# One pass of row sums moved into ScalarE's own order, and the place where the bound's broadcast line is read

## The chip, the cores and the metric

The kernel runs on one core of a Trainium2 chip. The time is device microseconds of the whole program, the median of several runs; lower is better. TensorE does the matrix products, VectorE and ScalarE the element work, GpSimd (POOL in the profile) a part of it and some DMA issues, SyncE (SP) most DMA issues.

## The reference, cut to what matters

A decoder trunk of two layers over 1024 tokens of width 1024, in float32.

```python
for layer in range(2):
    # layer 0: causal pooling; layer 1: forgetting attention over shared K/V
    h = x @ w_in                       # columns [main | mem q | main gate | mem gate]
    y = concat([main_fn(u) * silu(g_main), memory_attention(q_mem, mem, w_mem_kv) * silu(g_mem)])
    x = layer_norm(ALPHA * x + y @ w_out, ln_g, ln_b)
```

What the change touches lies in the output projection `y @ w_out` of layer 0, in the norm that follows it, and in the first part of layer 1, where the queries of its memory attention are made. In layer 1's forgetting attention the kernel scales q and k by powers of two before they become pairs of half-precision numbers. That scale needs an upper bound: the largest sum of absolute weights over 32 weight pieces (the key weights and layer 1's query weights), times a bound of the norm's output.

## The kernel before, in words

Each float32 product is made of three cheaper ones: an operand is split into a high part (`hi_lo`, line 163, on ScalarE), a low part (line 164, on VectorE, which needs the high part) and a rounded copy of the whole, "top" (line 165, on ScalarE).

**The output projection of layer 0** (`OutProj.rest`, lines 515 to 539) runs over four blocks of 256 tokens (`sp`), and in each over three groups of channels (`c` = 2, 0, 1). I call the twelve steps pieces 0 to 11: pieces 0 to 2 are the first block, 3 to 5 the second, and so on. A piece loads its activations from DRAM (line 533), splits them (lines 163 to 165, tiles `T`, six buffers shared by source, high and low/top) and then makes 48 products of 512 columns (line 496): two groups of 128 tokens by two halves of the columns, each a PSUM bank (`L`, three buffers, or `pj`, two) into which all three pieces of the block add. After the third piece VectorE reads the banks out (line 550) and the norm follows (`norm`, lines 541 to 566). Its rows are then transposed on TensorE for layer 1: 16 transposes per block (line 347), one behind every sixth product of the second and third piece of the block that follows (line 537). Four of them fill a PSUM bank `T` (two buffers), which lines 163 to 165 read out into `A`.

**The sums** (`look_ahead`, lines 190 to 202) are made meanwhile. Called from the loop of the products, it keeps three weight pieces on their way (line 194, a DMA issued by GpSimd into the ring `raw`, four buffers) and adds up the oldest one (line 200, an activation with an accumulator on ScalarE). Before the change it is called behind every 12th product, 32 times in all, and its activation is wrapped in an ordering relative to that product; a relation that the tool adds only to instructions on the product's own engine, TensorE. The order of ScalarE's queue is thus left to the scheduler. After the last piece `spread_bound` (lines 220 to 227) takes the largest per partition (line 223, VectorE), writes that column to DRAM (line 224, GpSimd) and reads it back as a row broadcast to all partitions (line 226, GpSimd) into a tile of the ring `raw`.

**The scales** (`scales_of`, lines 229 to 239) are ten small VectorE instructions; the first reads the broadcast row. In the code it is called in layer 1 behind the first head's queries (line 378), while the scheduler is free to place it.

The order on each engine's queue is the scheduler's, except on TensorE where parts are scheduled by hand, and where `keep_in_program_order` pins an instruction behind whatever was traced before it on its own engine. Each engine works off its queue in order: what stands behind a waiting instruction waits too.

Of the kernel before, what the change touches and what calls it, by code (L numbers as in the profile page):

```python
# [14 lines left out]
AF = mybir.ActivationFunctionType  # L15
ALU = mybir.AluOpType
AX = mybir.AxisListType

P = 128
# [54 lines left out]
def trunk_kernel(ctx, tc, x, xT, memT, win, wk, wv0, wv, wmk, wmv, wout, poolw, pscale, lng, lnb, bforget, out):  # L74
# [5 lines left out]
    nc = tc.nc  # L80
# [14 lines left out]
    def nm(tag):  # L95
        count[0] += 1
        return f"{tag}{count[0]}"

    def sb(shape, tag, bufs, dt=F32, where=None):
        return (where or pool).tile(shape, dt, tag=tag, name=nm(tag), bufs=bufs)  # L100
# [13 lines left out]
    def raw(shape):  # L114
        return sb(list(shape), "raw", 4)
# [38 lines left out]
    def three(a, b):  # L154
        return (a.hi, b.hi), (a.top, b.lo), (a.lo, b.top)
# [30 lines left out]
    rowsums = const.tile([P, NPIECES], F32, name="rowsums")  # L186
    to_see = [w[p, pc] for p in range(8) for w in (wk, win[1]) for pc in range(2)]
    landed, bound = [], []

    def look_ahead(after=None):  # L190

        while to_see and len(landed) < 3:
            r = raw([P, 4, P])
            nc.gpsimd.dma_start(r, to_see.pop(0))  # L194
            landed.append(r)
        if landed:
            k = NPIECES - len(to_see) - len(landed)
            r = landed.pop(0)
            with tc.issue_after(after):
                nc.scalar.activation(r, r, AF.Abs, accum_out=rowsums[:, k : k + 1])  # L200
        if not to_see and not landed and not bound:
            bound.append(spread_bound())

    scales = const.tile([P, 8], F32, name="scales")
    ex, ew, sq, unq, sqk, nsqk, tmp, tmp2 = (scales[:, k : k + 1] for k in range(8))

    def power_of(to, m, least):

        nc.vector.tensor_scalar(m, m, least, None, ALU.max)
        nc.vector.tensor_scalar(to.bitcast(I32), m.bitcast(I32), 0x7F800000, None, ALU.bitwise_and)  # L210
# [9 lines left out]
    def spread_bound():  # L220

        line = dram.tile([P, 1], F32, name=nm("line"))
        nc.vector.tensor_reduce(tmp, rowsums, AX.X, ALU.max)
        nc.gpsimd.dma_start(line, tmp)
        every = raw([P, P])
        nc.gpsimd.dma_start(every, line.rearrange("p o -> (p o)").partition_broadcast(P))
        return every

    def scales_of(every):

        nc.vector.tensor_reduce(tmp2, every, AX.X, ALU.max)
        power_of(ew, tmp2, 2.0 ** -24)
        nc.vector.tensor_tensor(ew, ew, ex, ALU.mult)
        nc.vector.reciprocal(sqk, ew)
        nc.vector.tensor_scalar(nsqk, sqk, -(2.0 ** 8), None, ALU.mult)
        nc.vector.tensor_scalar(sqk, sqk, 2.0 ** 8, None, ALU.mult)
        nc.vector.tensor_tensor(unq, ew, ew, ALU.mult)
        nc.vector.tensor_scalar(unq, unq, 2.0 ** -19, None, ALU.mult)
        nc.vector.reciprocal(sq, unq)
# [122 lines left out]
    def mem_attention(l, X, kv, qtile, ytile, yd):  # L362
# [6 lines left out]
        for h in range(MH):  # L369
            while turns:  # L370
                spread()
            q = parts_of(qtile, [P, S])
            run(slab(win[l, 8 + h], X, lambda cols, acc: hi_lo(q[:, cols], acc)))
            qs.append(q)
            if not l:
                keys(h)
            elif h == 0:
                scales_of(bound.pop())
            vals(h)
# [61 lines left out]
    class OutProj:  # L441
# [39 lines left out]
        def products(self, accs, c, ys, apart=False):  # L481

            high, low_top = (0,), (1, 2)
            if apart:
                order = [(a, nh, part) for a in range(2) for part in (high, low_top) for nh in range(2)]
            else:
                order = [
                    (a, nh, part) for part in ((low_top, high) if c == 0 else (high, low_top))
                    for a in range(2) for nh in range(2)
                ]  # L490
            for a, nh, part in order:
                for i in part:
                    for k in range(4):
                        kt = 4 * c + k
                        y, w = three(ys[:, k, a * P : (a + 1) * P], self.ws[nh][kt // 2][kt % 2])[i]
                        mm = nc.tensor.matmul(  # L496
                            accs[a][nh], y, w, start=kt == 8 and i == 0, stop=kt == 7 and i == 2,
                        )
                        self.done += 1
                        if not self.l and self.done % 12 == 7 and not bound:  # L500
                            look_ahead(mm.ins)
                        yield NH

        def early(self, y, ys):
# [592 lines left out]
```

## Time and profile before

| what | value |
|---|---|
| median of 3 runs | 1238.59 us (1235.18 to 1239.75) |
| the profiled execution's own time | 1231.11 us |
| span of its profile, first to last instruction | 1229.3 us |
| TensorE matmul busy | 1189.1 us, 97% of the span |
| VectorE busy | 781.2 us, 64% |
| ScalarE busy | 702.3 us, 57% |
| GpSimd busy | 239.2 us, 19% |
| mean granted TensorE clock | 0.99 |

The profile is of one execution, 7.5 us faster than the median of the three others. A row of its timeline gives the start, the duration, the engine, the line, the operation with its tiles and the count of merged instructions; in brackets stands how long the engine was idle before, and what released it. A row of a table by stretch gives the busy time of each engine in it, the granted clock (1.00 is full speed) and the share of the DMA engines.

### The profile page before, as it was taken

Reading aid. Unit: us, or ns where it says so; the run is one execution under the profiler, and the core shown is the slowest. Engines: PE = TensorE matmul, PEld = TensorE weight load, DVE = VectorE, ACT = ScalarE, POOL = GpSimd, SP = SyncE. Lnnn points to the kernel's source line nnn. Section 1 sums busy time; section 2 is a strip of 40 time slices with the busy share of each in tenths; the row PEclk is TensorE's granted clock in tenths of the full one; section 3 lists DMA queues with packets and bytes.
Section 4 is the critical chain, followed back from the end, with each engine's and each line's share of the span. In section 5 each row is a group of like instructions: output and inputs, shape, how many; then the busy total and the mean of one; then the engine's idle time right before and its main releaser. Section 6 shows DMA issues by size and latency. Waiting matters only on the chain. (4 is left out here: it accounts for less than half of the span.)

```text
span 1229.3 us, 20184 instructions
## 1 busy us (share of the span) xinstructions
PE 1189.1 (97%) x7018; PEld 729.0 (59%) x7018; DVE 781.2 (64%) x1839; ACT 702.3 (57%) x1508; POOL 239.2 (19%) x383
## 2 busy tenths in 40 slices
PE   8999999999988999999999999999999999999996
PEld 4566666555544566666786555556556555555553
DVE  7534676375724566346735787777877788774744
ACT  6555774374574335558623677666766676685220
POOL 4000000000031000000001444544444434650000
PEclk8999999999998999999999999999999999999999
DMA  6233564232586333326535799997998999996340
GB/s 224 86 115 93 121 136 137 86 121 95 185 279 188 129 120 101 102 85 123 109 112 120 166 174 198 200 175 165 205 201 161 207 185 222 233 232 212 131 142 35
DMA packets 272997, 187.79 MB, mean 153 GB/s; under 512 B 213424, under 2 KB 226864, under 8 KB 272896
## 3 DMA queue, kind: packets, MB, share of 16 engines
q1 hardware_dynamic: 270272, 178.06, 57.8%
q0 software_dynamic: 2624, 8.46, 2.1%
q8 instruction: 55, 0.90, 0.3%
q14 instruction: 46, 0.38, 0.1%
HBM read 103.43 MB, written 22.61 MB: 103 GB/s over the span
## 5 line engine op out<-in xcount | busy, mean ns | idle before, releaser
L267 PE MATMUL pj<-A,w 128*128 128x512 bf16 (+1 forms) x2928 | 690.0, 392 | 2.6 <-ACT A L163 2.3
L267 PEld LDWEIGHTS <-w 128*128 128x128 bf16 x1984 | 187.9, 98 | 221.0 <-issue 18.9
L267 PEld LDWEIGHTS pj<-A,w 128*128 128x128 f32 x976 | 180.9, 189 | 47.5 <-ACT A L163 3.9
L866 ACT ACTIVATE T<-MK,s 128x512 f32<-128x512 f32 x192 | 111.5, 581 | 54.1 <-DVE s L858 39.2
L888 DVE SCALAR_TENSOR_TENSOR P<-T,s,P 128x512 f16<-128x512 f32 x192 | 111.8, 613 | 39.6 <-ACT P L887 38.7
L887 ACT ACTIVATE P<-T,s 128x512 f16<-128x512 f32 x192 | 102.4, 576 | 59.6 <-issue 27.9
L164 DVE TENSOR_TENSOR w<-raw,w 128x512 bf16<-128x512 f32 x106 | 75.0, 709 | 83.2 <-PE pj L267 50.7
L496 PEld LDWEIGHTS <-T 128*128 128x128 bf16 x736 | 70.7, 98 | 83.8 <-issue 3.7
L244 PE MATMUL L<-B,B 128*128 128x512 f16 (+3 forms) x384 | 84.2, 327 | 6.3 <-DVE s L858 2.6
L858 DVE CUSTOM_DVE_ANT_0 MK<-L,R,scales 128x512 f32<-128x512 f32 (+3 forms) x128 | 80.3, 627 | 11.8 <-DMA R<-cumd 6.5
L163 ACT CAST w<-raw 128x512 fp32r<-128x512 f32 x106 | 65.9, 622 | 26.5 <-PE pj L267 14.5
L158 POOL TENSOR_SCALAR w<-raw 128x512 fp32r<-128x512 f32 x108 | 66.4, 622 | 71.7 <-DMA B<-B 44.9
L165 ACT CAST w<-raw 128x512 bf16<-128x512 f32 x106 | 65.8, 621 | 20.3 <-PE pj L267 19.7
L850 POOL TENSOR_SCALAR_AFFINE_SELECT R<-R 128x128 f32<-128x128 f32 x128 | 41.5, 330 | 164.4 <-DVE s L858 95.2
L169 POOL TENSOR_TENSOR w<-raw,w 128x512 bf16<-128x512 f32 x54 | 69.5, 1286 | 19.5 <-PE pj L267 17.3
L194 POOL DMA_DIRECT2D raw<-in_wk_dram x16 | 8.9, 559 | 330.4 <-DMA y0d<-Y 313.6
L164 DVE TENSOR_TENSOR T<-T,T 128x1024 bf16<-128x1024 f32 x23 | 28.0, 1217 | 66.6 <-ACT T L163 52.1
L244 PEld LDWEIGHTS <-B 128*128 128x128 f16 x384 | 34.0, 98 | 49.8 <-issue 12.7
L910 PE MATMUL O<-T,V 128*64 128x128 f16 (+1 forms) x1152 | 57.6, 220 | 4.5 <-DMA T<-P 4.2
L910 PEld LDWEIGHTS <-V 128*64 128x64 f16 (+1 forms) x1152 | 50.3, 104 | 18.3 <-issue 6.9
L496 PE MATMUL pj<-B,T 128*128 128x512 bf16 (+1 forms) x192 | 54.3, 392 | 4.5 <-DVE G L550 4.5
L163 ACT CAST T<-T 128x1024 fp32r<-128x1024 f32 x23 | 24.0, 1044 | 46.9 <-DMA T<-y1d 32.4
(250 smaller groups left out, 1710.0 us busy)
## 6 DMA issues: line engine op xcount, KB each, us to landing
raw<-in_win_dram SPq DMA_DIRECT2D x96, 256.0 KB, 2.8
raw<-in_wout_dram SPq DMA_DIRECT2D x40, 256.0 KB, 2.8
B<-B SPq DMA_DIRECT2D x69, 128.0 KB, 3.2
R<-cumd SPq DMA_DIRECT2D x16, 512.0 KB, 4.3
y0d<-Y SPq DMA_DIRECT2D x12, 512.0 KB, 2.9
T<-y0d SPq DMA_DIRECT2D x12, 512.0 KB, 4.9
T<-y1d SPq DMA_DIRECT2D x11, 512.0 KB, 4.6
raw<-in_wmk_dram SPq DMA_DIRECT2D x16, 256.0 KB, 2.6
```

The costliest lines, as they stand in the source:

```text
L158: nc.gpsimd.tensor_scalar(to, src, 1.0, 1.0, ALU.mult, ALU.mult)
L163: pin(nc.scalar.copy(to.hi, src))
L164: pin(nc.vector.tensor_tensor(to.lo, src, to.hi.bitcast(F32), ALU.subtract))
L169: nc.gpsimd.tensor_tensor(to.lo, src, to.hi.bitcast(F32), ALU.subtract)
L244: nc.tensor.matmul(acc, a, b, start=i == 0, stop=i == len(terms) - 1)
L267: nc.tensor.matmul(accs[n], a[:, k, :], b[:, pc * 4 + k, n * NH : (n + 1) * NH], start=seen[n] == 1, stop=seen[n] == 3 * KT,)
L496: mm = nc.tensor.matmul(accs[a][nh], y, w, start=kt == 8 and i == 0, stop=kt == 7 and i == 2,)
L858: nc.vector.tensor_tensor_reduce(p[:, lo:up], lg, R[:, lo:up], unq, top, ALU.add, ALU.min, m[:, n : n + 1])
L866: nc.scalar.activation(e, p[:, lo:up], AF.Exp, bias=top, scale=-1.0, accum_out=sums[:, n, hd % 2, i : i + 1],)
L887: nc.scalar.activation(pair[:, lo:up], e, AF.Copy, scale=r)
L888: nc.vector.scalar_tensor_tensor(pair[:, L + lo : L + up], e, r, pair[:, lo:up], ALU.mult, ALU.subtract)
L910: nc.tensor.matmul(acc[rows, (i % 4) * P : (i % 4) * P + P], v[:, b, 2 * j : 2 * j + (1 if e else 2), :].rearrange("p e d -> p (e d)"), pt ...
```

## The change

Three edits, and no instruction more or less on any engine.

1. The sums are called behind every 16th product in place of every 12th, and each is pinned on ScalarE behind what was traced there before it (`keep_in_program_order` in place of `issue_after`).
2. The broadcast row lands in the ring `P` (four buffers, used by the norm's two vectors here and by the memory's softmax later) in place of the ring `raw`.
3. The first instruction of `scales_of` is pinned on VectorE behind what was traced before it, which is the first head's queries of layer 1's memory attention.

```diff
-    def look_ahead(after=None):
+    def look_ahead():
...
-            with tc.issue_after(after):
-                nc.scalar.activation(r, r, AF.Abs, accum_out=rowsums[:, k : k + 1])
+            tc.keep_in_program_order(nc.scalar.activation(r, r, AF.Abs, accum_out=rowsums[:, k : k + 1]))
...
         nc.gpsimd.dma_start(line, tmp)
-        every = raw([P, P])
+        every = sb([P, P], "P", 4)
         nc.gpsimd.dma_start(every, line.rearrange("p o -> (p o)").partition_broadcast(P))
...
     def scales_of(every):
-        nc.vector.tensor_reduce(tmp2, every, AX.X, ALU.max)
+        tc.keep_in_program_order(nc.vector.tensor_reduce(tmp2, every, AX.X, ALU.max))
...
-                        mm = nc.tensor.matmul(
+                        nc.tensor.matmul(
                             accs[a][nh], y, w, start=kt == 8 and i == 0, stop=kt == 7 and i == 2,
                         )
                         self.done += 1
-                        if not self.l and self.done % 12 == 7 and not bound:
-                            look_ahead(mm.ins)
+                        if not self.l and self.done % 16 == 7 and not bound:
+                            look_ahead()
                         yield NH
```

In the built program the change of order reaches from the first output-projection pieces to layer 1's first queries: ScalarE's queue between its 356th and 428th instruction, VectorE's between its 375th and 538th, and with them the order of some of SyncE's and GpSimd's DMA issues. TensorE's queue is the same, instruction by instruction, and behind that stretch all queues are the same too.

## The prediction

> **What bounds the kernel now.** I read the page first, then the table by stretch around the output projection of layer 0, then the timelines of the engines there.
>
> ```profile
> span 1229.3 us, 20184 instructions
> PE 1189.1 (97%) x7018; PEld 729.0 (59%) x7018; DVE 781.2 (64%) x1839; ACT 702.3 (57%) x1508; POOL 239.2 (19%) x383
> ```
>
> TensorE has work 97% of the span and no other engine comes near it. So the time is TensorE's products plus the places where it stands still or runs slowly. By stretch:
>
> ```profile
> 364.00:375.00 11.00, 6.47 (x20) 4.22 (x19) 6.55 (x10) 7.48 (x19) 3.83 (x7) 0.69 0.76 248
> 394.00:405.00 11.00, 4.34 (x14) 3.10 (x13) 3.78 (x13) 2.02 (x3) 0.55 (x1) 0.69 0.27 75
> 413.00:447.00 34.00, 34.00 (x164) 20.25 (x163) 19.17 (x36) 11.24 (x17) 0.00 (x0) 1.00 0.33 108
> 481.00:505.00 24.00, 20.05 (x141) 14.62 (x141) 16.18 (x34) 16.81 (x37) 0.00 (x0) 1.00 0.40 133
> ```
>
> The columns behind the stretch are its length, then the busy time of PE, PEld, DVE, ACT and POOL, the granted clock and the DMA share. Two stretches have holes, and in both the clock is down to 0.69; later the same kind of work fills 34.00 of 34.00. TensorE's timeline gives what the holes cost:
>
> ```profile
> 363.71 1.27 PE L496 MATMUL L<-B,T 128*128 128x512 f32 x4
> 369.51 2.08 PE L496 MATMUL pj<-B,T 128*128 128x512 f32 x4 [4.53 <-DVE G L550]
> 371.38 1.91 PE L496 MATMUL L<-B,T 128*128 128x512 f32 x4
> 373.09 1.62 PE L496 MATMUL pj<-B,T 128*128 128x512 f32 x4
> ...
> 381.47 0.59 PE L496 MATMUL L<-W,T 128*128 128x512 bf16 x2
> ...
> 392.86 0.71 PE L496 MATMUL L<-Y,T 128*128 128x512 f32 x2
> ...
> 401.13 0.47 PE L347 MATMUL T<-ident,G 128*128 128x128 f32 x1 [6.66 <-ACT A L165]
> ...
> 412.88 1.18 PE L496 MATMUL L<-B,T 128*128 128x512 f32 x4
> ...
> 423.68 0.59 PE L496 MATMUL L<-W,T 128*128 128x512 bf16 x2
> ...
> 435.06 0.71 PE L496 MATMUL L<-Y,T 128*128 128x512 f32 x2
> ...
> 446.56 1.18 PE L496 MATMUL L<-B,T 128*128 128x512 f32 x4
> ```
>
> These are starts of pieces: 3 at 363.71, 4 at 381.47, 5 at 392.86, 6 at 412.88, 7 at 423.68, 8 at 435.06, 9 at 446.56. Piece 3 takes 17.76 us, its undisturbed twin 6 takes 10.80: **6.96 lost**. Piece 5 takes 20.02, its twin 8 11.50: **8.52 lost**. Piece 4 takes 11.39 against piece 7's 11.38: nothing. The change can give back at most 15.5 us here. The row 481 to 505 has 3.95 us of further holes, on layer 1's first weights; the change moves nothing there.
>
> **Why piece 5 stops.**
>
> ```profile
> 385.16 0.19 DVE L223 TENSOR_REDUCE scales<-rowsums 128x1 f32<-128x32 f32 x1 [0.63 <-ACT raw L200]
> 398.37 0.29 DVE L231 TENSOR_REDUCE scales<-raw 128x1 f32<-128x128 f32 x1 [13.03 <-DMA raw<-line]
> ...
> 399.79 0.67 DVE L164 TENSOR_TENSOR A<-T,A 128x512 bf16<-128x512 f32 x1
> ...
> 400.50 0.58 ACT L165 CAST A<-T 128x512 bf16<-128x512 f32 x1 [11.07 <-DVE A L164]
> ...
> 385.75 0.54 POOL L224 DMA_DIRECT2D line<-scales  x1 [4.95 <-DVE scales L223]
> 395.24 0.55 POOL L226 DMA_DIRECT2D raw<-line  x1 [8.94 <-issue]
> ```
>
> The scheduler put the scales' first instruction right behind the reduction whose result has to go to DRAM and back. VectorE waits 13.03 us for the row (385.75 out, 395.24 back, 398.37 landed). Behind it stands line 164 of a transposed bank, at 399.79, behind that ScalarE's line 165 at 400.50, which frees the bank, and TensorE's next transpose, at 401.13, needs the bank.
>
> **Why piece 3 stops.**
>
> ```profile
> 355.18 1.04 ACT L163 CAST T<-T 128x1024 fp32r<-128x1024 f32 x1
> ...
> 357.36 1.03 ACT L165 CAST T<-T 128x1024 bf16<-128x1024 f32 x1
> ...
> 364.63 0.63 ACT L200 ACTIVATE raw<-raw 128x512 f32<-128x512 f32 x1 [2.86 <-DMA raw<-in_wk_dram]
> ...
> 365.26 1.03 ACT L163 CAST T<-T 128x1024 fp32r<-128x1024 f32 x1
> ...
> 356.25 1.23 DVE L164 TENSOR_TENSOR T<-T,T 128x1024 bf16<-128x1024 f32 x1 [4.71 <-ACT T L163]
> 366.32 1.23 DVE L164 TENSOR_TENSOR T<-T,T 128x1024 bf16<-128x1024 f32 x1 [8.84 <-ACT T L163]
> ...
> 368.79 0.67 DVE L550 SCALAR_TENSOR_TENSOR G<-G,pj 128x512 f32<-128x512 f32 x1
> ...
> 372.32 0.68 DVE L550 SCALAR_TENSOR_TENSOR G<-G,pj 128x512 f32<-128x512 f32 x1
> ...
> 358.41 0.52 SPq L533 DMA_DIRECT2D T<-y0d  x1
> ```
>
> The banks `pj` of block 0 are read out at 368.79 and 372.32, behind a line 164 for piece 4 that waited 8.84 us for ScalarE's high part at 365.26. That high part waited for its source, issued at 358.41, as soon as piece 3's top (357.36 + 1.03) had freed the buffer, and at the end for a sum that itself waited 2.86 us for its weights.
>
> **The change part by part.** By the order of the built program:
>
> *The scales (edit 3)* move behind line 164 of the first head's queries, in layer 1, and VectorE goes from the norm straight to the transposed banks. The 13.03 us wait goes. What is late next: the bank, filled when piece 4 ends, waits for at most four sums, two casts and its own three copies. Sums, casts and the landing of their loads:
>
> ```profile
> L200 ACT ACTIVATE raw<-raw 128x512 f32<-128x512 f32 x32 | 20.0, 626 | 15.2 <-DMA raw<-in_wk_dram 8.2 <-DMA raw<-in_win_dram 6.9
> L200 ACT ACTIVATION_READ_ACCUMULATOR raw<-raw 128x1 f32 x32 | 6.0, 186 | 0.0
> DMA to landing us min/median/max: 2.8/3.4/7.3
> DMA to landing us min/median/max: 5.2/6.0/8.4
> ```
>
> (The third row is of the sums' loads, line 194; the fourth of the loads into `T` between 340 and 372 us.) A sum costs ScalarE 626 + 186 ns = 0.81 us. A bank holds four transposes, one behind every sixth product, and there are two: the second is full 24 products (5.7 us at 11.50/48) behind the first and is needed again 30 products (7.2 us) later. From the first bank's filling ScalarE and VectorE copy it (0.58 + 0.67 + 0.58), add the first sum (0.81), which frees the buffer for the fourth's load (0.55 to issue, 3.4 to land), and add the fourth (0.81): 7.4 us, 1.7 behind the second bank's filling. Then come that bank's own copies and a cast between them, 1.83 + 1.04. Together 4.6 of the 7.2: no stop. **Saved: 8.5 us**. With the slowest landing of the row, 7.3 in place of 3.4, it would be 1.3 less.
>
> At its new place the ten instructions take 399.79 - 398.37 = 1.42 us, in front of the read-out of head 0's values:
>
> ```profile
> 513.59 0.48 DVE L338 SCALAR_TENSOR_TENSOR MK<-pj,s,MK 128x256 f16<-128x256 f32 x1 [0.54 <-ACT MK L337]
> 510.97 10.84 PE L267 MATMUL pj<-A,w 128*128 128x512 f32 x48
> ```
>
> That read-out ends at 514.07, and the bank is needed at the second half of the 48 products, 510.97 + 5.42 = 516.39. With 1.42 added 0.9 us are left: cost nothing. The row has landed long before: its DMAs, 13 us as above, are issued at the end of block 2, three pieces (33.7 us) and layer 1's first weights ahead. Without that cover: up to 1.4 us.
>
> *The sums (edit 1).* One fewer stands ahead of piece 3's high part, and none between it and its top. The high part comes at 355.18 - 0.81 = 354.4; line 164 follows it by 1.07 and takes 1.23 (rows at 355.18 and 356.25), so the source buffer is free at 356.7 in place of 358.4. I take the median landing, 6.0: piece 4's high part starts at **362.7** in place of 365.26. The three sums in front of it are no hindrance (3 x 0.81, on loads that I count as issued by 355 and landed 3.4 later). From there the rows count on: the second `pj` bank was free for TensorE 373.09 - 365.26 = 7.83 later, and then 36 of the 48 products are left, 36 x 10.80/48 = 8.1 at full speed. Piece 4 starts at 362.7 + 7.83 + 8.1 = 378.6 in place of 381.47. **Saved: 2.8**; with a landing of 5.2 it is 3.6, with 8.4 it is 0.4. I take off 0.1 for a reciprocal that now stands ahead of the second read-out: 2.7.
>
> The other sums spread over pieces 4 to 9. Some 20 x 0.81 = 16.2 us come to ScalarE, over some 70 us of which in the undisturbed part 11.24 of 34 were busy. Each stands behind work that the next step needs anyway. The banks `pj` at the ends of blocks 1 and 2 hang on VectorE behind ScalarE's copies; adding up the same durations I find about 1 us of slack and take nothing, bounds 0 and +1 each. The memory's tokens load later than before (their buffers are the sums'), still ahead of their first cast.
>
> *The ring (edit 2).* `P` has a free buffer at that time (weights in one, the norm's vectors in two), so the row waits for none; and the tokens' fourth load no longer waits for the scales. Nothing.
>
> Sum: -8.5 - 2.7 = **-11.2 us**. For the profiled execution, 1231.11, that is 1219.9; its lead of 7.5 us on the median of the three runs is no part of the change, so I forecast 1238.59 - 11.2 = **1227.4**.
>
> **The clock.** In the trace holes of 4.53 and 6.66 us are followed by 0.69, while the stretch of 3.95 us in several holes kept 1.00. My piece 3 has two holes left, from 364.98 (363.71 + 1.27) to 362.7 + 4.25 = 366.95 (the first bank, 369.51 - 365.26 later) and, two groups of 0.9 later, from 368.75 to 370.5: 2.0 and 1.8, so I take full speed. [...]
>
> **The rivals.**
> 1. *Piece 3 stays cold.* The group behind the last hole then takes what such a group took, 373.09 - 371.38 = 1.71 in place of 0.9, and the next as much. Price 0.8 to 1.6: 1228 to 1229. [...] Against: 1.00 at 481 to 505.
> 2. *Half the gain goes into new waits of ScalarE.* Each of some 20 sums can wait for its load with casts behind it. At the slow landing a bank is 1.3 late (above); at five banks and two block ends that is 9.1: 1227.4 + 9.1 = 1236.5, within 0.5% of before. For it: sums waited 15.2 us for loads in all. Against: those loads ran behind each other at a DMA share of 0.76; spread out they meet 0.33.
> 3. *The stop of piece 3 repeats (slower).* It was a cast behind a waiting sum, with the banks' read-out behind that. Pinned sums now stand ahead of casts at the ends of all blocks. If that holds line 550 at three ends of blocks, at 6.96 each with the cold clock, 20.9 come back against 8.5 saved: 1238.59 + 12.4 = 1251. It decides from where a load takes longer than its lead, three sums of 16 products, 10.8 us. Against: the longest took 7.3.
> 4. *It doesn't do what it says*: pins that the scheduler evades. The built order excludes it for the scales; small, and counted with rival 2.
>
> **How the numbers follow.** Half a percent, 6.2 us, is about what a measurement of this kernel tells from no change. Chances: forecast 0.66, rival 1 0.10, rivals 2 and 4 0.17, of which a third still saves over 6.2, rival 3 0.07. So faster 0.82, same 0.11, slower 0.07. The range takes the landing from 5.2 to 8.4 (-12.0 to -8.8), the runs' spread (-3.4, +1.2), and reaches into rival 2: 1223 to 1235.
>
> **What would show it.** In the profile of the changed kernel: the scales' first reduction behind 490 us with no wait for the row; piece 5 in about 11.5 us; no transpose that waits for line 165; piece 3 in about 14.9 with two holes under 2.3 us and a clock near 1.00; no `pj` wait at the ends of blocks 1 and 2. Wrong would be: ScalarE idle on weights with line 163 behind it, and TensorE waiting for a bank at pieces 6, 9 or at 481 us.

## The result, and the profile after

The changed kernel takes **1220.70 us** (median of 4 runs, 1218.72 to 1226.01) against 1238.77 for the kernel before beside it (4 runs, 1235.18 to 1239.75): ratio 0.9866, 95% interval 0.9829 to 0.9903. The forecast was 1227.4 with a range down to 1223.0: the direction is right, the gain of 18.1 us is larger than the 11.2 forecast, and the time lies 2.3 us below the range. The two profiled executions differ by less, 9.95 us (1231.11 to 1221.16).

The page of the changed kernel:

```profile
span 1219.4 us, 20174 instructions
PE 1186.1 (97%) x7018; PEld 726.4 (60%) x7018; DVE 781.4 (64%) x1839; ACT 701.2 (57%) x1508; POOL 238.8 (20%) x383
```

The counts on the five engines are those of before; the ten instructions fewer in the first row are among those that do not count as busy.

The same stretches as in the prediction's table (length, busy time of PE, PEld, DVE, ACT, POOL, granted clock, DMA share, GB/s):

```profile
364.00:375.00 11.00, 9.93 (x45) 5.59 (x44) 10.86 (x22) 6.11 (x13) 2.12 (x4) 1.00 0.39 143
394.00:405.00 11.00, 11.00 (x54) 6.59 (x52) 10.29 (x21) 6.02 (x14) 1.64 (x3) 1.00 0.49 172
413.00:447.00 34.00, 34.00 (x164) 20.26 (x162) 19.01 (x34) 16.39 (x33) 2.73 (x5) 1.00 0.51 137
481.00:505.00 24.00, 22.63 (x126) 14.40 (x126) 10.78 (x31) 13.71 (x28) 0.00 (x0) 1.00 0.36 109
```

Of the two stops one hole of 1.07 us is left, and the clock of 0.69 is gone. The undisturbed stretch is still full with ScalarE at 16.39 instead of 11.24: part of the sums now lies there. TensorE's timeline, starts of pieces 3 to 6:

```profile
365.59 1.27 PE L495 MATMUL L<-B,T 128*128 128x512 f32 x4
369.75 1.20 PE L495 MATMUL pj<-B,T 128*128 128x512 f32 x4 [1.07 <-DVE G L549]
377.71 0.59 PE L495 MATMUL L<-W,T 128*128 128x512 bf16 x2
389.09 0.71 PE L495 MATMUL L<-Y,T 128*128 128x512 f32 x2
400.59 1.18 PE L495 MATMUL L<-B,T 128*128 128x512 f32 x4
```

Piece 3 takes 12.12 us (17.76 before), piece 5 11.50 (20.02). But piece 3 starts 1.88 us later than before (365.59 against 363.71). That is no sign of a cost: in three further profiles of the kernel before, pieces 0 to 2 are as slow as here (first column of the table below), and its first profile is the exception. The scales are read far behind, with no wait in brackets:

```profile
497.41 0.28 DVE L230 TENSOR_REDUCE scales<-P 128x1 f32<-128x128 f32 x1
```

From the starts, piece 6 begins 12.29 us earlier (412.88 to 400.59), and the spans differ by 9.9. Of the 2.4 us lost in between, 1.7 lie at one spot of layer 1. In the kernel before, TensorE's timeline has there

```profile
685.59 0.38 PE L244 MATMUL L<-B,B 128*128 128x256 f16 x2 [2.03 <-DVE s L858]
685.80 2.32 PE L267 MATMUL pj<-A,w 128*128 128x512 bf16 x10
```

and in the changed kernel

```profile
674.56 0.38 PE L243 MATMUL L<-B,B 128*128 128x256 f16 x2 [2.00 <-DVE s L857]
674.78 3.90 PE L266 MATMUL pj<-A,w 128*128 128x512 bf16 x10
```

The same hole of 2.0 us, and behind it ten products in 2.32 or in 3.90 us: the clock fell in one execution and not in the other (0.72 between 674 and 680 us in the changed kernel, 1.00 between 684 and 692 in the kernel before). None of the three edits touches that place; the last section shows where the two differ. So one profile of each kernel doesn't settle the size; more were needed.

### The profile page after: what moved, and what is told of

The parts are those of the page before. It is cut to its first block, busy times and chain, and to the rows that moved or that the text cites. A ratio compares the mean times of both kernels' runs of the same rounds, so it can differ in the third digit from the quotient of the medians.

```text
span 1219.4 us, 20174 instructions
## 1 busy us (share of the span) xinstructions
PE 1186.1 (97%) x7018; PEld 726.4 (60%) x7018; DVE 781.4 (64%) x1839; ACT 701.2 (57%) x1508; POOL 238.8 (20%) x383
```

## The experiments

Each time is a median, each ratio against the kernel before on the same chip (1233.0 to 1234.4 us in these comparisons). Pieces are read from the starts on TensorE's timeline (where a trace lacks some records, counted from their neighbours):

| us | pieces 0-2 | 3 | 4 | 5 | 6 | 9 |
|---|---|---|---|---|---|---|
| before | 32.62 | 17.76 | 11.39 | 20.02 | 10.80 | 10.68 |
| before_again | 35.77 | 13.93 | 11.70 | 21.54 | 10.68 | 10.67 |
| before_third | 34.55 | 17.79 | 11.41 | 18.30 | 10.68 | 10.67 |
| before_fourth | 34.80 | 15.59 | 11.90 | 21.89 | 10.68 | 10.67 |
| after | 34.73 | 12.12 | 11.38 | 11.50 | 10.68 | 10.67 |
| after_again | 36.51 | 10.76 | 11.41 | 11.50 | 10.67 | 10.67 |
| after_third | 34.12 | 11.80 | 11.42 | 11.49 | 10.68 | 10.67 |
| sums_only | 34.34 | 11.47 | 11.42 | 11.49 | 10.68 | 10.67 |
| scales_ring | 36.50 | 13.49 | 11.38 | 16.53 | 10.68 | 10.67 |
| sums16_free_all | 36.35 | 14.19 | 11.50 | 16.08 | 10.66 | 10.67 |
| sums12_all | 33.72 | 15.00 | 11.39 | 11.50 | 12.63 | 16.30 |
| scales_ring_norow | 35.93 | 13.38 | 11.42 | 11.49 | 10.73 | 10.68 |
| sums12_norow | 34.12 | 14.31 | 11.42 | 11.49 | 14.83 | 10.68 |
| after_row2 | 34.95 | 12.34 | 11.42 | 13.56 | 14.74 | 10.67 |
| no_sums | 32.26 | 12.78 | 11.42 | 11.49 | 10.68 | 10.67 |
| late_sums | 32.20 | 10.76 | 11.41 | 11.50 | 12.02 | 12.16 |
| from48_pe15 | 31.69 | 10.90 | 11.42 | 11.49 | 10.92 | 11.69 |
| from48_pe15_again | 31.87 | 10.80 | 11.41 | 11.50 | 11.18 | 11.36 |

### Both kernels again, and single edits

My first theory was the prediction's: edit 3 frees piece 5, edit 1 piece 3, and the clock adds some. Its rivals were chance, and stops that vary.

**before_again** (no edit). 

> The kernel before, unchanged, to learn what differs from one execution to the next. The profiled execution of before (1231.11 us) lay 7.5 us under the median of its timed runs (1238.59), that of after (1221.16) beside its own median (1220.70). Theory A (clock): the stops of pieces 3 and 5 leave TensorE at a granted clock of 0.5 for longer in some executions than in others, each stretch of 6.83 us at 0.5 costing up to 3.4; it expects executions from 1231 to 1240, with the mean clock falling by about 0.0014 for each 3.4 us stretch, so 0.990 at 1231 and 0.984 or less at 1239. Theory B (the stops themselves): the row of sums or the weights of the sums land later in other executions; it expects stops of pieces 3 and 5 that differ by several us in this profile from 17.76 and 20.02, at a clock of 0.99. Theory C (noise of both kernels): the gap between the kernels falls to 10 to 12 us with more runs.

1233.93 us, ratio 0.9993 (0.9982 to 1.0004). The stops vary as theory B said, piece 3 13.93 for 17.76 and piece 5 21.54 for 20.02, but not by much in sum. Theory A is right that the slower executions have the lower clock: of 63 later executions of the kernel before, the nine with a mean clock of 0.985 to 0.987 took 1236.7 us on average, the fourteen with 0.992 to 0.994 took 1232.7. But the first profile's 0.990 is an ordinary value, so A does not explain its lead. What fell is the median: 1234.38 beside this run, where the first comparison had 1238.77.

**after_again** (no edit). 

> The changed kernel, unchanged, on the same chip as the kernel before again. Theories A and B expect 1219 to 1222 us, ratio 0.985 to 0.988, and a spread smaller than before's; theory C 1225 to 1228, ratio 0.990 to 0.992. All expect piece 3 in 12 to 13 us and piece 5 in 11.5.

1218.44 us, ratio 0.9874 (0.9854 to 0.9895): 15.9 us, as theories A and B had it and not the 10 to 12 of theory C. Piece 3 takes 10.76, less than all three expected.

**sums_only**: edit 1 alone.

```diff
-            with tc.issue_after(after):
-                nc.scalar.activation(r, r, AF.Abs, accum_out=rowsums[:, k : k + 1])
+            tc.keep_in_program_order(nc.scalar.activation(r, r, AF.Abs, accum_out=rowsums[:, k : k + 1]))
...
-                        if not self.l and self.done % 12 == 7 and not bound:
+                        if not self.l and self.done % 16 == 7 and not bound:
```

> Edit 1 alone: sums behind every 16th product and pinned, the scales where the scheduler puts them and the row in ring raw. By the built order the scales' first reduction then stands in the norm behind block 3, ahead of layer 1. Piece 3 should take 12 to 13 us as in after, piece 5 11.5. If the row has landed by then, this edit alone gives the whole gain: 1219 to 1223, ratio 0.985 to 0.988. If it is as late as it was (13 us of wait), the stop moves to the end of block 3 and costs 5 to 9 there: 1226 to 1231, ratio 0.990 to 0.994.

1219.95 us, ratio 0.9879 (0.9860 to 0.9899). Edit 1 alone gives what all three give. VectorE still waits for the row, 5.78 us, in the norm behind block 2, and nothing on TensorE is late for it.

```profile
446.46 0.28 DVE L230 TENSOR_REDUCE scales<-raw 128x1 f32<-128x128 f32 x1 [5.78 <-DMA raw<-line]
```

**scales_ring**: edits 2 and 3 alone.

```diff
-        every = raw([P, P])
+        every = sb([P, P], "P", 4)
...
-        nc.vector.tensor_reduce(tmp2, every, AX.X, ALU.max)
+        tc.keep_in_program_order(nc.vector.tensor_reduce(tmp2, every, AX.X, ALU.max))
```

> Edits 2 and 3 alone: the scales' first reduction pinned in layer 1 and the row in ring P; the sums stay behind every 12th product, not pinned. All theories expect piece 5 in 11.5 us without a wait for line 165, and piece 3 in 17 to 18 as before. By the forecast's terms 8.5 us faster than before, ratio 0.993; by theory A the clock lost after that stop comes on top where it strikes: 9 to 12 faster, ratio 0.990 to 0.993.

1228.51 us, ratio 0.9954 (0.9940 to 0.9968): less than half the gain, and **piece 5 still takes 16.53**, which no theory had expected (nor piece 3 in 13.49). VectorE no longer waits for the row. ScalarE does; its timeline, then TensorE's, then the DMA issues between 392 and 403 us (last column: us from issue to landing):

```profile
392.70 0.59 ACT L163 CAST A<-T 128x512 fp32r<-128x512 f32 x1
400.77 1.04 ACT L163 CAST T<-T 128x1024 fp32r<-128x1024 f32 x1 [7.48 <-DMA T<-y0d]
401.72 0.58 ACT L165 CAST A<-T 128x512 bf16<-128x512 f32 x1
```

```profile
402.35 0.33 PE L347 MATMUL T<-ident,G 128*128 128x128 f32 x1 [3.13 <-ACT A L165]
```

```profile
T<-y0d SPq DMA_DIRECT2D x1, 512.0 KB, 7.9
G<-in_x_dram SPq DMA_DIRECT2D x1, 512.0 KB, 8.6
P<-line POOLq DMA_DIRECT2D x1, 64.0 KB, 4.9
```

The bank's copy, line 165, stands on ScalarE behind the cast of piece 6's activations, and that load took 7.9 us. In the changed kernel, between 420 and 432 us, such loads take half:

```profile
T<-y0d SPq DMA_DIRECT2D x2, 512.0 KB, 3.9
```

### What delays the load

What runs beside it is the row's write to DRAM, 128 values of 4 bytes. In scales_ring the write is issued first, and 9.6 us pass until it has landed; the load goes out in that time:

```profile
387.33 0.55 POOL L224 DMA_DIRECT2D line<-scales  x1 [6.49 <-DVE scales L223]
```

```profile
392.83 0.53 SPq L533 DMA_DIRECT2D T<-y0d  x1
```

In the kernel before, the DMA issues between 384 and 399 us were:

```profile
raw<-in_memT_dram SPq DMA_DIRECT2D x4, 256.0 KB, 9.2
x<-G SPq DMA_DIRECT2D x1, 512.0 KB, 9.7
...
line<-scales POOLq DMA_DIRECT2D x1, 0.5 KB, 8.8
```

The store and three of the four loads, all issued within 1.2 us of the write, land when it does, between 394.2 and 395.5. In the changed kernel the write (GpSimd, first row) goes out behind the last load of `y0d` (SyncE, second row), since the sums, pinned and 16 products apart, are done later; what it delays there is the residual's load, which has time:

```profile
432.61 0.54 POOL L223 DMA_DIRECT2D line<-scales  x1 [9.85 <-DVE s L553]
```

```profile
428.23 0.53 SPq L532 DMA_DIRECT2D T<-y0d  x1
```

```profile
G<-in_x_dram SPq DMA_DIRECT2D x1, 512.0 KB, 10.7
...
line<-scales POOLq DMA_DIRECT2D x1, 0.5 KB, 8.4
```

Four kernels part edit 1 and the sums' own cost.

**sums12_all**: all three edits, but `self.done % 12 == 7`. 

> The changed kernel with the sums behind every 12th product in place of every 16th, pinned. It parts edit 1 into the place and the spacing. If the pin carries the gain (a sum can no longer stand ahead of a cast with its weights not landed), 1218 to 1222 us, ratio 0.986 to 0.990, and piece 5 in 11.5. If the spacing carries it (sums at every 12th hold ScalarE on their loads, so that the source of the next piece is freed and loaded late), piece 5 stays at 15 to 17 us as with edits 2 and 3 alone, and piece 3 at 13 to 14: 1226 to 1229 us, ratio 0.993 to 0.996.

1230.66 us, ratio 0.9986 (0.9972 to 1.0001). The gain is gone, though piece 5 takes 11.50: pieces 3, 6 and 9 stop. Neither of the two cases expected it. At piece 9's stop the write is again beside the load; the issues between 424 and 437 us:

```profile
T<-y0d SPq DMA_DIRECT2D x1, 512.0 KB, 10.4
G<-in_x_dram SPq DMA_DIRECT2D x1, 512.0 KB, 10.0
...
line<-scales POOLq DMA_DIRECT2D x1, 0.5 KB, 8.3
```

The sums are done earlier, the write goes out at 425.20, and the load of `y0d` issued at 425.54 is the one that it meets.

**sums16_free_all**: all three edits, but the activation under `issue_after` as before, not pinned. 

> The changed kernel with the sums behind every 16th product but not pinned: the other half of edit 1. If the spacing carries the gain, 1218 to 1222 us, ratio 0.986 to 0.990, piece 5 in 11.5. If the pin does, a stop of piece 3 or 5 of 3 to 9 us is left: 1222 to 1229, ratio 0.990 to 0.996.

1229.21 us, ratio 0.9962 (0.9948 to 0.9976). Without the pin the scheduler moves the sums ahead again, the write goes out at 387.28, and piece 5 takes 16.08. So neither the place nor the spacing carries the gain alone: together they put the write behind the last load.

**no_sums**: the sums and their loads left out. A constant stands in place of their results; the row still goes through DRAM. 

> The changed kernel without the 32 sums and their loads (the row is filled with a constant instead, so the scales are not those of the weights). It shows what the sums still cost where they now stand. If pieces 0 and 1 (13.2 to 14.1 and 10.6 to 12.2 us in four of the five profiles so far, 11.7 and 10.6 in that of before) are late because the sums' loads run beside those of y0d, they take 11.5 to 12 and 10.6 here, piece 3 10.7, and the kernel 1213 to 1216 us (ratio 0.983 to 0.985). If they are late for another reason, the time stays at 1217 to 1220 (ratio 0.986 to 0.988), as in the changed kernel.

1219.90 us, ratio 0.9886 (0.9871 to 0.9901): the whole time is no shorter without the sums. Yet piece 0 falls to 11.33, as expected if the sums' loads delay it; where that gain goes is shown at from48_pe15 below. The write goes out at 338.31 here, beside block 0's loads, so piece 3 is no clean reading, and the run does not tell what the sums cost by themselves.

**late_sums**: the changed kernel with `self.done > 144 and self.done % 12 == 7`. 

> The changed kernel with no sum in block 0: they begin behind product 151, one behind every 12th, pinned. Block 0 then has no loads of sums beside those of y0d. If those loads delay pieces 0 and 1, these take 11.5 to 12 and 10.6 us, and the time is 1214 to 1217, ratio 0.983 to 0.986, faster than the changed kernel. If a sum behind every 12th product is too dense wherever it stands, the pieces of blocks 1 and 2 stop as those of before did, 3 to 5 us each: 1220 to 1227, ratio 0.988 to 0.994. If neither, as the changed kernel: 1217 to 1220.

1227.01 us, ratio 0.9946 (0.9934 to 0.9958), in a way that none of the cases had. Block 0 is faster, pieces 6 and 9 lose 1.3 and 1.5 us, and the write, now at 453.39, meets layer 1's first weights (issues between 452 and 469 us). ScalarE waits for these, VectorE's read-out of the last banks stands behind their split, and TensorE waits for the read-out: it is busy 19.91 of 23 us from 447 to 470, against 22.88 in after_third.

```profile
raw<-in_wmk_dram SPq DMA_DIRECT2D x7, 256.0 KB, 9.3
```

```profile
466.09 0.62 ACT L163 CAST w<-raw 128x512 fp32r<-128x512 f32 x1 [7.09 <-DMA raw<-in_wmk_dram]
469.87 5.58 PE L300 MATMUL pj<-T,w 128*128 128x256 f32 x33 [2.97 <-DVE G L549]
```

Two theories are left for the late load: the write holds the other transfers up (W), or the loads of the sums and the memory do (L). Three kernels tell them apart.

**scales_ring_norow**: scales_ring without the row's two transfers, a constant in the row's place.

```diff
-        nc.gpsimd.dma_start(line, tmp)
         every = sb([P, P], "P", 4)
-        nc.gpsimd.dma_start(every, line.rearrange("p o -> (p o)").partition_broadcast(P))
+        nc.vector.memset(every, 40.0)
```

> Edits 2 and 3 alone (1228.51 us, piece 5 in 16.53) without the row's two transfers: the row is a constant in its place, so the scales are not those of the weights. In nine of the ten profiles so far a load issued while the row's write to DRAM is under way (8 to 10 us from issue to landing) lands 8 to 11 us after its issue, in place of 3.8 to 6. Theory W (the write holds the other transfers up): the load of y0d issued at 392.8 lands in 4 to 5 us, ScalarE's copy of the transposed bank behind it is in time, piece 5 takes 11.5, and the kernel 1223 to 1225 us, ratio 0.991 to 0.993. Theory L (the sums' own loads and the memory's delay that load): piece 5 stays at 15 to 17, 1227 to 1229 us, ratio 0.994 to 0.996.

1225.00 us, ratio 0.9940 (0.9924 to 0.9955), a time at the end of W's range and a ratio at the end of L's, so the whole time does not decide. Piece 5 does: it takes 11.49 in place of 16.53, with the load issued at 392.80, where it was in scales_ring. Between 392 and 403 us:

```profile
T<-y0d SPq DMA_DIRECT2D x2, 512.0 KB, 3.9
G<-in_x_dram SPq DMA_DIRECT2D x1, 512.0 KB, 5.4
```

**sums12_norow**: the same edit in sums12_all. 

> All three edits with the sums behind every 12th product, pinned (1230.66 us; pieces 3, 6 and 9 in 15.0, 12.6 and 16.3), without the row's two transfers, a constant in its place. Its write was issued at 425.2, the load of y0d at 425.5 landed after 10.4 us, and piece 9 stopped. Theory W expects piece 9 in 10.7 to 12.6 (the spacing's own loss of pieces 3 and 6 stays), 1225 to 1227 us, ratio 0.992 to 0.995. Theory L expects 1229 to 1232 as before.

1226.64 us, ratio 0.9955 (0.9942 to 0.9969), as W had it: piece 9 falls from 16.30 to 10.68. Pieces 3 and 6 still stop (14.31 and 14.83), with no write beside them: the spacing's own cost. Ahead of piece 6 a sum that waited 2.67 us for its weights stands before ScalarE's casts; the chain from there is not followed further. Piece 6 is slower than in sums12_all (12.63), with a hole of 2.32 us.

**after_row2**: a second write of 128 values, read by nobody.

```diff
+            if k == 16:
+                nc.gpsimd.dma_start(dram.tile([P, 1], F32, name=nm("second")), rowsums[:, k : k + 1])
```

> The changed kernel with a second write of 128 values of 4 bytes to DRAM, issued behind sum 16 (385.4 us in the changed kernel), just ahead of the load of y0d at 387.0; nobody reads it. Theory W expects that load to land 8 to 10 us after its issue in place of 4.3, ScalarE's cast of it and the bank's copy behind it to come 4 to 6 us late, piece 5 in 15 to 17 in place of 11.5, and 1222 to 1225 us, ratio 0.990 to 0.993. Theory L expects no difference from the changed kernel: 1217 to 1221, ratio 0.986 to 0.989.

1223.49 us, ratio 0.9925 (0.9912 to 0.9937), against 0.9874 without it: W's time. The write went out one load earlier than I had meant, at 374.34, and met the load of 374.81. The issues between 374 and 390 us, ScalarE's wait, and the stretch behind the write:

```profile
T<-y0d SPq DMA_DIRECT2D x1, 512.0 KB, 12.5
x<-G SPq DMA_DIRECT2D x1, 512.0 KB, 11.8
second<-rowsums POOLq DMA_DIRECT2D x1, 0.5 KB, 8.4
```

```profile
387.70 1.05 ACT L163 CAST T<-T 128x1024 fp32r<-128x1024 f32 x1 [13.77 <-DMA T<-y0d]
```

```profile
377.00:380.00 3.00, 3.00 (x16) 1.41 (x14) 0.00 (x0) 0.00 (x0) 0.00 (x0) 1.00 1.34 56
```

The same stretch of the changed kernel, without that write:

```profile
377.00:380.00 3.00, 3.00 (x17) 1.44 (x15) 0.01 (x1) 0.00 (x0) 0.00 (x0) 1.00 0.85 286
```

The last two columns are what to read: the DMA engines show more time in packets (a share of 1.34 for 0.85) and move a fifth of the bytes (56 GB/s for 286). Pieces 5 and 6 lose 2.06 and 4.07 us, where W had expected the whole loss in piece 5. The sums' and the memory's loads were there without this write too, so theory L is out as the cause. Nor is it the issuing engine: GpSimd issues the 32 loads of the sums as well, and `y0d` beside those lands in 6.6 us or less behind 360 us. Why a write of such small pieces does this, no run shows.

### A better version, and what was left of the size

**from48_pe15**: the changed kernel with no sum in piece 0, one behind every 15th product from 48 on, and the row without DRAM.

```diff
-        line = dram.tile([P, 1], F32, name=nm("line"))
...
+        wide = sb([P, P], "P", 4)
+        nc.vector.tensor_copy(wide, tmp.to_broadcast([P, P]))
+        def across():
+            bank = ps([P, 4, P], "T", 2)
+            nc.tensor.transpose(bank[:, 0, :], wide, ident)
+            nc.vector.tensor_reduce(tmp2, bank[:, 0, :], AX.X, ALU.max)
+        turns.append(across)
...
+                        if not self.l and self.done > 48 and self.done % 15 == 7 and not bound:
```

> A version that might beat the changed kernel: no sums in piece 0 (from product 48 on, one behind every 15th, pinned), so that piece 0 keeps the 11.3 us that it has without the sums (13.4 to 14.1 with them); and the row by a transpose on TensorE with the maximum read from its bank, without DRAM, since the sums end later (product 517) and a write then would meet layer 1's weights. If piece 0 keeps its gain and the later pieces stay full, 1214 to 1217 us, ratio 0.983 to 0.986. If the sums' loads delay the y0d loads of pieces 2 to 4 in place of those of piece 0, or the memory's first loads come late, the gain goes there: 1217 to 1221, ratio 0.986 to 0.989.

**from48_pe15_again**, beside after_third. 

> The version with no sum in piece 0 and the row by a transpose, beside the changed kernel on one chip. If the 3.4 us that its profile gained in the out projection are there in every execution, 3 us under after_third, ratio 0.003 lower. If piece 0's gain depends on the execution, or is lost behind the out projection, within 1.5 us of after_third.

**after_third**. 

> The changed kernel, unchanged, beside the version from product 48 on. 1218 to 1221 us, ratio 0.986 to 0.990; pieces 0 to 5 in 69.5 to 70.5 us as in its two profiles (69.7 and 70.2).

1217.53 us, ratio 0.9877 (0.9864 to 0.9890); again 1219.40, 0.9889 (0.9869 to 0.9910), beside 1219.13, 0.9890 (0.9867 to 0.9913) for after_third. So it is no faster, the second case of both expectations; after_third's pieces 0 to 5 took 68.83 us, a little under what was expected. Pieces 0 to 2 do gain, 31.69 us for 34 to 36; TensorE then comes early to the transposes ahead of layer 1 and waits there. Its timeline, and the stretch:

```profile
473.87 1.61 PE L350 MATMUL T<-ident,G 128*128 128x128 f32 x8 [2.83 <-DVE G L566]
```

```profile
470.00:481.00 11.00, 8.17 (x58) 7.12 (x56) 9.44 (x28) 9.05 (x20) 0.00 (x0) 0.84 0.44 167
```

The clock is down to 0.84 behind the hole. In no_sums it is 0.84 too, behind a hole of 2.28 us, while after_third has 1.00 behind one of the same 2.28; the last section shows where they differ. Beside after_third, pieces 0 to 5 gain 3.3 us, pieces 6 to 9 lose 1.3 of it (table), and from the start of piece 10 to a run of 20 products in layer 1 (at 481.75, in after_third at 482.02) it takes 39.35 us for 38.23, 1.1 more. What is left, about 1 us, is within what executions differ by.

**before_third**, **before_fourth** (no edit). 

> The kernel before, unchanged: a third profile of it. If other executions lose more at the stops than the two profiled ones, pieces 0 to 5 together take more than 82.9 us here (81.8 and 82.9 so far), up to 86. If they do not, 81 to 83, and what is missing lies behind the out projection or in the sample.

> As before_third, a fourth profile: more than 82.9 us for pieces 0 to 5 if other executions lose more there, 81 to 83 if not.

One execution each took 1230.50 and 1236.18 us. Pieces 0 to 5 take 82.05 and 84.18 us, one as the first profiles and one above. Over four profiles of before they take 82.74 on average (81.79, 82.93, 82.05, 84.18), over three of after 69.58 (69.73, 70.18, 68.83): **13.2 us** of gain are located.

## Why the prediction was right or wrong

- *Piece 5, saved 8.5.* Right in size: 20.44 on average of four profiles to 11.50, 8.9. Wrong in cause: it was put down to edit 3 alone, "late next is the bank", with "four sums, two casts and its own three copies". With edits 2 and 3 alone 5.0 us of the stop stay (16.53 for 11.50), because late next is the load of piece 6, whose cast stands on ScalarE ahead of the bank's line 165. The prediction had followed the row's DMAs (13 us) only as a wait, not as traffic that others wait behind. Edit 1, costed at nothing for this piece, frees it, and does so without edit 3 too (sums_only, 11.49).
- *Piece 3, saved 2.7.* The steps hold: the fourth load was forecast to bring its cast to 362.7 us and it came at 361.87. But piece 3 then took 12.12, not 14.9, because it began 1.88 us later: the lead of the loads over TensorE is what counts, and what pieces 0 to 2 lose, piece 3 doesn't. So the four go together: 50.70 us on average before (50.38, 49.69, 52.34, 50.39), 46.68 after (46.85, 47.27, 45.92), 4.0 saved.
- *Sums spread, 0; scales' new place, 0; ring, 0.* Right: the stretch 413 to 447 is full, TensorE waits for nothing between 375 and 470 us, and sums_only, with the row in `raw`, equals the changed kernel.
- *Rivals 2 and 3* did not come, but sums12_all is close to rival 3: pinned sums with a shorter lead stop pieces 3 and 6 at two of the ends that it named. The price there was 2 to 4 us each, not 6.96.
- *The clock* kept 1.00 in piece 3, as forecast, but the ground given, that its two holes are of 2.0 and 1.8 us, does not hold: behind one of 2.00 us it was 0.50 for 3.4 us (the changed kernel, from 675.4 us). Elsewhere it differs from one execution to the next (means of 0.985 to 0.994 in the 63 later executions of the kernel before), which the sum left out.

**Two steps failed.** *In the mechanism* it is the step from "The 13.03 us wait goes" to "no stop", which gave the whole of piece 5 to edit 3. The runs showed in its place that edit 3 alone leaves 5.0 us, behind a load that the row's write holds up (7.9 us beside the write, a median of 3.9 without it), and that edit 1 alone takes all of it away: the write goes out behind the last load, and VectorE's wait for the row comes where nothing hangs on it. That 8.5 was near 8.9 is luck: the change has both edits. All the signs of being right that the prediction named came true, save piece 3's length and second hole, and none of them could tell one edit from the other.

*In the number* it is the last step, from the sum to the time and the range. The sum was 11.2, where the profiles locate 13.2: 0.4 short in piece 5 and 1.3 in pieces 0 to 3, the rest in piece 4. That alone stays within the range (1238.59 - 13.2 = 1225.4). What took the time out of it is the base: "its lead of 7.5 us on the median of the three runs is no part of the change". It set 1238.59 as the kernel before's time, from three runs, with only their spread in the range. The first comparison has those three and one more, 1238.77 in the middle, three of the four above 1238; of 63 later executions one was. In the later comparisons the median of before was 1233.0 to 1234.4 (8 to 16 runs each), from which the sum gives 1221.8 to 1223.2, and the gain was 15.9 and 13.9 us, not 18.1. All three intervals allow 13.2 to 16. What the first comparison had in addition, 2.2 to 4.2 us, and the 0.7 to 2.7 us between the profiles' 13.2 and the later medians, no run places: executions of one kernel differ by 5 us and more (1230.50 to 1236.18), some of it by chance holes like the one at 674 us. That stays open.

## What to carry to other kernels

When a wait goes, list for each engine behind it what stands next in its queue, loads included, and ask what else was in the air at that time: here the row's way through DRAM was not only 13.03 us of wait for its reader, but its write also held up a neighbour, a load of 7.9 us in place of 3.9. Put a write like this one (0.5 KB, 8.8 us to landing in the kernel before) where no needed load is issued beside it, or do without DRAM. Where a change has several edits, test each alone before a sum that came out is taken for a cause that was right. And take a forecast's base from as many executions as can be had: three runs and one profile that disagree by 7.5 us are a range, not a point.

## What the runs showed of the hardware

A write of 128 values of 4 bytes to DRAM took 6.6 to 12.0 us from issue to landing in the 14 profiles that have one. While such writes were under way, 35 loads and stores of 256 or 512 KB were issued. Every one of them landed behind the write, 0.3 to 6.5 us later, and 5.6 to 13.3 us after its own issue; a load of `y0d` away from the write, behind 360 us, takes 3.7 to 6.6. No run here shows why the write is slow or why its neighbours wait.

A hole of 2.0 us on TensorE was followed by full speed in one execution and by half clock in another. The clock records of the 18 traces show where they differ. Between 20 and 1195 us all stretches at half clock last 3.41 us or a whole multiple of it, and within a trace they begin on one grid of 3.41 us: in the kernel before 6.83 us from 367.25 and again from 397.96, nine steps later; in the changed kernel 3.41 us from 675.36. I divided TensorE's time into windows of that grid. At full clock, 34 windows had 2.0 us or more of idle time, and each was followed by half clock; of some 6100 windows with less than 1.94 us, none was (in between, two were and one was not). In the first profiles of the two kernels alone it is three of three, and none of 678. The two holes of the result's section, with the windows on both sides (TensorE's busy time is the first figure behind the length). In the changed kernel the hole lies in one window:

```profile
671.90:675.30 3.40, 1.40 (x9) 0.72 (x8) 2.71 (x8) 2.97 (x7) 0.01 (x1) 1.00 0.62 169
675.40:678.70 3.30, 3.30 (x9) 1.22 (x8) 2.91 (x9) 2.46 (x6) 0.88 (x2) 0.50 0.53 108
```

In the kernel before it is split between two, and the clock stays:

```profile
681.30:684.70 3.40, 2.26 (x11) 0.98 (x10) 2.00 (x5) 1.72 (x3) 0.84 (x3) 1.00 0.72 179
684.70:688.10 3.40, 2.51 (x13) 1.27 (x13) 3.25 (x11) 2.59 (x7) 0.88 (x2) 1.00 0.44 116
```

So it is with the holes of 2.28 us: in no_sums, with 0.84 from 470 to 481 us, one window holds the whole of it; in after_third, with 1.00, it is split. The prediction's hole of 4.53 us was at half clock from 367.2 us on, 2.3 us after its beginning.
